# Stick-breaking branch: the fp16 split of a chunk is written over its own U tile, four U tiles and three hlT tiles in place of three and two

## The chip, the cores and the metric

The kernel runs on one core of one Trainium2 chip. The metric is the time of one execution on the device in microseconds, as the median of several runs. Before the change three runs took 2247.16, 2248.38 and 2257.34 us; the median is 2248.38 us.

## The reference, cut to what matters

```python
def reference(x, ...):                                   # x: (1, 2048, 1024) float32
    h = rmsnorm(x, norm_in_g)
    q_sb, k_sb, v_sb, gate_sb, c_q, c_kv, k_rope, gate_mla, gate_logits = split(h @ w_in)
    # first branch: 8 heads of 64, blocks of 128 queries, strictly causal
    z = q k^T * 64 ** -0.5
    w = exp(log_sigmoid(z) + sum of log_sigmoid(-z) over the keys between s and t)
    o_sb = w @ v
    # second branch (MLA): 8 heads, low-rank q and kv, rope, softmax over chunks of 64
    o_mla = softmax(q_full k_full^T * 96 ** -0.5) @ v_mla
    y = g_sb * ((o_sb * silu(gate_sb)) @ w_o_sb) + g_mla * ((o_mla * silu(gate_mla)) @ w_o_mla)
    return rmsnorm(x + y @ w_out, norm_f_g)
```

The first branch's weight of key s for query t is sigmoid(z_ts) times the product of 1 - sigmoid(z_tj) over the keys j between them. The rows of x are handed over in reverse order, so that this product runs forward.

## The kernel before

Every factor of a matmul is kept as two fp16 halves, hi and lo (hi is the value rounded, lo the rest), and a product is three matmuls: hi*hi, hi*lo, lo*hi. The kernel has these stages.

*Norm.* `norm_x` (line 214) loads a block of 128 rows into a U or a B tile, scales it, splits it into hi and lo and has SP transpose it into `hT` (line 223). The split lies in an `hl` tile for even blocks and in an `hlT` tile for odd ones.

*Heads.* 16 heads follow each other, eight of the first branch (`sb_units`, line 344) and eight of the second (`mla_units`, line 527). Beside them `dense_stream` is advanced: units of 24 matmuls (line 166 to 168) that project x onto the next heads' q, k and v, onto the second branch's low-rank factors, and onto the gates. PLAN says how many units go with a head: 17 with each of the first eight heads, then 8, and 4 with the last.

A head of the first branch has 16 units of 128 queries, and a unit one or two chunks of up to 1024 keys, 24 chunks a head. A chunk passes through these steps:

- TensorE writes the scores z (line 332) into one of two PSUM tiles.
- GpSimd sets U[:, 0] to 1 (line 359); ScalarE writes U = sigmoid(-z) (line 360) and B = sigmoid(z) (line 361).
- `stick`: VectorE scans U to running products (line 364; the second chunk of a unit starts from the last column of the first one's U, `unit["prev"]`) and multiplies B by U (line 367).
- `weigh`: ScalarE casts B to hi (line 370) and VectorE subtracts to get lo (line 371), both into an `hl` tile; SP transposes `hl` into an `hlT` tile (line 278).
- `values`: TensorE multiplies the transposed weights by v (lines 287 to 290), and ScalarE copies the sum out after a unit's last chunk.

The second branch has the same last two steps; its chunk is scaled (line 558), exponentiated (line 568), cast (line 571) and subtracted (line 572).

The code is written so that the steps of several chunks overlap: `second` holds back a chunk's `stick` (or `softmax`) until the next chunk's scores are written, and `third` holds back its `values`. `run_third(keep)` in `weigh` leaves `keep` of them, so with 1 the values of chunk j are written down when chunk j + 2 is split, with 2 when j + 3 is. A planner with a model of the engines' times then orders each engine's instructions and gives each new tile the next free buffer of its tag; an instruction that needs a buffer waits for the last user of the one that it gets.

The tiles of 4 KB a partition: three U, three B, two `hl` and two `hlT` in the pool `un`. After the second branch's projections (in head 4) weights' memory comes free and the pool `more` gives three `hl` and three `hlT` on top, and `weigh` keeps 2 instead of 1; `count` deals the requests to the two pools. Before the last head `more` is closed, and its memory goes to the tail's first tiles.

*Tail.* `gated`, `merge` and `finish` weigh both branches by the gates, multiply by the output matrices and norm. The first `gated(0)` is issued inside the last head, after unit EARLY.

Of the kernel before, what the change touches and what calls it, by code (L numbers as in the profile page):

```python
# [9 lines left out]
F32 = mybir.dt.float32  # L10
# [6 lines left out]
P = 128  # L17
# [12 lines left out]
MASK = -3.0e35  # L30
PLAN = [17] * 8 + [8] * 7 + [4]
SCALES = ("g", 4)
EARLY = 6
LEAD = 7
FIRST = 0

# [1 line left out]
def block_kernel(tc, x, norm_in_g, w_in, w_ck, b_gate, q_norm_g, w_q_up, kv_norm_g, w_kv_up,  # L38
# [11 lines left out]
    with ExitStack() as ctx:  # L50
# [121 lines left out]
        with ExitStack() as tctx:  # L172
# [24 lines left out]
            junk = rows.tile([P, WB], mybir.dt.bfloat16, name="junk", bufs=1)  # L197

            def u_tile():
                return un.tile([P, 1032], F32, name="U", tag="U")  # L200

            def b_tile():
                return un.tile([P, 1024], F32, name="B", tag="B")

            def hl_tile(n):
                count[0] += 1
                pool, bufs = (more[0], 3) if more and count[0] % 5 % 2 == 0 else (un, 2)
                return pool.tile([P, 2048], F16, name="hl", tag="hl", bufs=bufs)[:, 0:2 * n]

            def hlT_tile():  # L210
                pool, bufs = (more[0], 3) if more and count[0] % 5 % 2 == 0 else (un, 2)
                return pool.tile([P, 16, 128], F16, name="hlT", tag="hlT", bufs=bufs)

            def norm_x(i):
                xt = (b_tile() if i % 2 else u_tile())[:, 0:1024]
                SP.dma_start(out=xt, in_=x[i * P:(i + 1) * P, :])
                hl = (hlT_tile().rearrange("p a c -> p (a c)") if i % 2 else hl_tile(1024))
                ssq = sm.tile([P, 1], F32, name="ssq", tag="ssq")
                f = sm.tile([P, 1], F32, name="f", tag="f")
                A.activation(out=hl[:, 0:1024], in_=xt, func=AF.Square, accum_out=ssq)  # L220
                inv_rms(ssq, HS ** -2 / D, EPS * HS ** -2, f)
                split(xt, f, hl[:, 0:1024], hl[:, 1024:2048])
                SP.dma_start_transpose(out=hT[i // 8][:, :, i % 8 * P:(i % 8 + 1) * P], in_=hl)
# [43 lines left out]
                while len(second) > keep:  # L267
                    second.popleft()()

            def weigh(unit, vt, blk0, n, first, last, fill, done):  # L270


                run_third(2 if more else 1)
                hl = hl_tile(n)
                fill(hl[:, 0:n], hl[:, n:2 * n])
                nb = n // P
                t = hlT_tile()
                SP.dma_start_transpose(out=t[:, 0:2 * nb, :], in_=hl)

                def values():  # L280
                    if first:
                        unit["av"] = ps_av()
                    av = unit["av"]
                    with tc.issue_after(last_pe[0].ins):
                        for j in range(nb):
                            v = vt[blk0 // 8][:, blk0 % 8 + j, :]
                            T.matmul(out=av[:, 0:64], lhsT=t[:, j, :], rhs=v[:, 0:64],  # L287
                                     start=(first and j == 0), stop=False)
                            T.matmul(out=av[:, 0:64], lhsT=t[:, j, :], rhs=v[:, 64:128], start=False, stop=False)  # L289
                            T.matmul(out=av[:, 0:64], lhsT=t[:, nb + j, :], rhs=v[:, 0:64],  # L290
                                     start=False, stop=(last and j == nb - 1))
                    if last:
                        done(av)

                third.append(values)
# [48 lines left out]
            def sb_units(h, pre):  # L344
                zc, nzc, of = pre[2:5]
                kt, vt = kv_tiles(qk_d[h // 2][:, h % 2], v_d[h // 2][:, h % 2])
                put = o_group(h * 64)
                for i in range(NB):
                    if i % 4 == 0:
                        qt4 = kvp.tile([P, 3, 4, 128], F16, name="qt", tag="qt", bufs=2)  # L350
                        load_q(qk_d[h // 2][:, 2 + h % 2, i:i + 4], qt4[:, 0], qt4[:, 1])
                    unit = {}
                    cks = chunks(i)
                    for ci, (c0, n) in enumerate(cks):
                        z = ps_z()
                        scores(z, kt, [qt4[:, 0, i % 4, :], qt4[:, 1, i % 4, :]], i + c0 // P, n,
                               strict if ci == 0 else None)
                        U, B = u_tile(), b_tile()
                        G.memset(U[:, 0:1], 1.0)
                        A.activation(out=U[:, 1:n + 1], in_=z[:, 0:n], func=AF.Sigmoid, scale=nzc)  # L360
                        A.activation(out=B[:, 0:n], in_=z[:, 0:n], func=AF.Sigmoid, scale=zc)  # L361

                        def stick(U=U, B=B, n=n, ci=ci, c0=c0, i=i, unit=unit, last=(ci == len(cks) - 1)):
                            V.tensor_tensor_scan(out=U[:, 0:n + 1], data0=U[:, 0:n + 1], data1=U[:, 0:n + 1],  # L364
                                                 initial=unit["prev"] if ci else PS, op0=ALU.mult, op1=ALU.bypass)
                            unit["prev"] = U[:, n:n + 1]
                            V.tensor_tensor(out=B[:, 0:n], in0=B[:, 0:n], in1=U[:, 0:n], op=ALU.mult)  # L367

                            def fill(hi, lo):
                                A.copy(out=hi, in_=B[:, 0:n])  # L370
                                V.tensor_tensor(out=lo, in0=B[:, 0:n], in1=hi, op=ALU.subtract)  # L371

                            weigh(unit, vt, i + c0 // P, n, ci == 0, last, fill, lambda av: put(av, of, i))

                        second.append(stick)
                        run_second(1)
                    yield
# [156 lines left out]
            def mla_units(h, pre):  # L534
# [5 lines left out]
                for i in range(NB):  # L540
# [23 lines left out]
                    def softmax(cks=cks, zs=zs, ls=ls, nb=nb, unit=unit, i=i):  # L564
                        f = sm.tile([P, 1], F32, name="fo", tag="fo")
                        for ci, (c0, n) in enumerate(cks):
                            Z = zs[ci]
                            A.activation(out=Z[:, 0:n], in_=Z[:, 0:n], func=AF.Exp, bias=nb, accum_out=ls[:, ci:ci + 1])  # L568

                            def fill(hi, lo, Z=Z, n=n):  # L570
                                A.activation(out=hi, in_=Z[:, 0:n], func=AF.Copy, scale=PS)
                                V.scalar_tensor_tensor(out=lo, in0=Z[:, 0:n], scalar=PS, in1=hi,
                                                       op0=ALU.mult, op1=ALU.subtract)

                            weigh(unit, vt, i + c0 // P, n, ci == 0, ci == len(cks) - 1, fill,
                                  lambda av: put(av, f, i))
                        if len(cks) == 2:
                            V.tensor_tensor(out=ls[:, 0:1], in0=ls[:, 0:1], in1=ls[:, 1:2], op=ALU.add)
                        V.reciprocal(out=f, in_=ls[:, 0:1])
# [319 lines left out]
```

## Time and profile before

| what | us |
|---|---|
| median of three runs | 2248.38 |
| the profiled execution, its time | 2248.75 |
| its span, first to last instruction | 2247.0 |
| TensorE busy with matmuls | 1893.7 |
| VectorE busy | 1560.2 |
| ScalarE busy | 1236.7 |
| GpSimd busy | 300.0 |

All times below are of the profiled execution, in us from its first instruction. PE is TensorE, DVE VectorE, ACT ScalarE, POOL GpSimd, SP the engine that only issues DMAs; `L287` is line 287. "A <- B" in a list of waits says that A was idle and that the end of B released it. Five stretches are named by letters: A is 112 to 512.6 us (heads 0 to 2 of the first branch), B 512.6 to 862.7 (heads 3 and 4, beside the second branch's projections), C 862.7 to 1181 (heads 5 to 7), D 1181 to 1785 (heads 0 to 6 of the second branch), E 1785 to 1904 (its last head). The tail follows.

### The profile page before, as it was taken

Reading aid. Unit: us, or ns where it says so; the run is one execution under the profiler, and the core shown is the slowest. Engines: PE = TensorE matmul, PEld = TensorE weight load, DVE = VectorE, ACT = ScalarE, POOL = GpSimd, SP = SyncE. Lnnn points to the kernel's source line nnn. Section 1 sums busy time; section 2 is a strip of 40 time slices with the busy share of each in tenths; the row PEclk is TensorE's granted clock in tenths of the full one; section 3 lists DMA queues with packets and bytes.
Section 4 is the critical chain, followed back from the end, with each engine's and each line's share of the span. In section 5 each row is a group of like instructions: output and inputs, shape, how many; then the busy total and the mean of one; then the engine's idle time right before and its main releaser. Section 6 shows DMA issues by size and latency. Waiting matters only on the chain.

```text
span 2247.0 us, 41328 instructions
## 1 busy us (share of the span) xinstructions
PE 1893.7 (84%) x15776; PEld 1107.1 (49%) x15776; DVE 1560.2 (69%) x2692; ACT 1236.7 (55%) x2180; POOL 300.0 (13%) x668
## 2 busy tenths in 40 slices
PE   2978888789767888789898987878899986999997
PEld 1545555455434545456555554545556553444443
DVE  3368878778866869888887765656576766666664
ACT  5446656555655658676765665556565655322221
POOL 1211112111101111111111111111111110000000
PEclk9999999999978999999999999988999997999999
DMA  9988898888989979996879999999999989776752
GB/s 247 225 142 166 160 155 157 149 157 170 193 169 165 189 166 190 144 169 140 165 170 174 192 196 188 194 196 197 163 206 184 243 166 228 211 207 186 203 155 73
DMA packets 923431, 401.63 MB, mean 179 GB/s; under 512 B 860000, under 2 KB 880224, under 8 KB 921184
## 3 DMA queue, kind: packets, MB, share of 16 engines
q1 hardware_dynamic: 900640, 339.72, 77.3%
q0 software_dynamic: 20480, 58.74, 11.1%
q8 instruction: 123, 2.02, 0.4%
q10 hardware_dynamic: 2112, 0.52, 0.2%
q14 instruction: 76, 0.62, 0.1%
HBM read 132.52 MB, written 71.84 MB: 91 GB/s over the span
## 4 chain that ended last, share of the span: by engine, by line
DMA 35%; PE 35%; DVE 14%; issue 7%; ACT 7%; SPq 1%; POOL 0%; DVEq 0%; ACTq 0%; POOLq 0%
DMA hlT<-hl 20%; PE z L332 6%; PE mm L166 5%; DVE U L364 5%; PE mm L167 5%; PE mm L168 4%; DMA rt<-r 3%; DMA utb<-hlb 2%; PE yo L166 2%; DMA wf<-in_w_in_dram 2%; PE yo L167 2%; PE yo L168 2%; DVE B L367 2%; PE av L287 2%; DVE hl L371 2%
## 5 line engine op out<-in xcount | busy, mean ns | idle before, releaser
L166 PE MATMUL mm<-w,hT 128*128 128x384 f16 (+1 forms) x1792 | 594.5, 332 | 68.6 <-ACT w L154 36.9
L167 PE MATMUL mm<-w,hT 128*128 128x384 f16 (+1 forms) x1792 | 594.4, 332 | 1.6 <-DVE w L155 1.5
L168 PE MATMUL mm<-w,hT 128*128 128x384 f16 (+1 forms) x1792 | 593.0, 331 | 0.0
L287 PE MATMUL av<-vt,hlT 128*128 128x64 f16 x2176 | 241.7, 198 | 213.9 <-DMA hlT<-hl 208.9
L364 DVE TENSOR_TENSOR_SCAN U<-U 128x1025 f32<-128x1025 f32 (+3 forms) x192 | 323.8, 1687 | 51.8 <-ACT U L360 51.3
L332 PE MATMUL z<-kt,qt 128*128 128x512 f16 (+3 forms) x1280 | 326.3, 361 | 22.9 <-DMA kt<-qkd 7.1
L287 PEld LDWEIGHTS <-hlT 128*128 128x128 f16 x2176 | 202.8, 101 | 268.6 <-DMA hlT<-hl 250.7
L370 ACT CAST hl<-B 128x1024 f16<-128x1024 f32 (+3 forms) x192 | 153.1, 798 | 226.0 <-DVE B L367 144.7
L166 PEld LDWEIGHTS <-hT 128*128 128x128 f16 x1792 | 179.8, 100 | 162.7 <-issue 29.3
L167 PEld LDWEIGHTS <-hT 128*128 128x128 f16 x1792 | 179.6, 100 | 142.6 <-issue 41.1
L290 PE MATMUL av<-vt,hlT 128*128 128x64 f16 x2176 | 241.1, 198 | 0.0
L289 PE MATMUL av<-vt,hlT 128*128 128x64 f16 x2176 | 241.0, 198 | 0.0
L168 PEld LDWEIGHTS <-hT 128*128 128x128 f16 x1792 | 179.5, 100 | 122.1 <-issue 16.0
L371 DVE TENSOR_TENSOR hl<-B,hl 128x1024 f16<-128x1024 f32 (+3 forms) x192 | 174.1, 908 | 83.2 <-ACT hl L370 82.7
L289 PEld LDWEIGHTS <-hlT 128*128 128x128 f16 x2176 | 202.5, 101 | 17.3 <-issue 1.6
L290 PEld LDWEIGHTS <-hlT 128*128 128x128 f16 x2176 | 202.9, 101 | 0.0
L332 PEld LDWEIGHTS <-qt 128*128 128x128 f16 x1600 | 141.1, 101 | 122.3 <-issue 24.0
L367 DVE TENSOR_TENSOR B<-B,U 128x1024 f32<-128x1024 f32 (+3 forms) x192 | 175.1, 912 | 15.7 <-ACT B L361 0.6
L360 ACT ACTIVATE U<-z,nzc 128x1024 f32<-128x1024 f32 (+3 forms) x192 | 166.5, 867 | 33.8 <-PE z L332 32.1
L361 ACT ACTIVATE B<-z,zc 128x1024 f32<-128x1024 f32 (+3 forms) x192 | 166.6, 867 | 0.0
L568 ACT ACTIVATE U<-U,nb 128x1024 f32<-128x1024 f32 (+7 forms) x128 | 98.4, 769 | 108.4 <-DVE nb L562 106.1
L558 DVE TENSOR_SCALAR_CACHE_REDUCE U<-z,mzc 128x1024 f32<-128x1024 f32 (+7 forms) x128 | 104.0, 814 | 60.4 <-PE z L332 59.4
(240 smaller groups left out, 3180.9 us busy)
## 6 DMA issues: line engine op xcount, KB each, us to landing
gd<-go POOLq DMA_DIRECT2D x128, 192.0 KB, 4.8
wf<-in_w_in_dram SPq DMA_DIRECT2D x26, 768.0 KB, 5.6
gt<-gd SPq DMA_DIRECT2D x10, 1024.0 KB, 6.1
qkd<-rt POOLq DMA_DIRECT2D x32, 256.0 KB, 4.2
mqd<-rt SPq DMA_DIRECT2D x32, 256.0 KB, 3.1
qt<-mqd POOLq DMA_DIRECT2D x32, 256.0 KB, 5.4
wf<-in_w_out_dram SPq DMA_DIRECT2D x16, 512.0 KB, 5.8
xt<-in_x_dram SPq DMA_DIRECT2D x16, 512.0 KB, 3.5
```

The lines of the kernel that those rows point to most:

```text
L166: T.matmul(out=ps, lhsT=xh(k), rhs=wh(k), start=(k == 0), stop=False)
L167: T.matmul(out=ps, lhsT=xh(k), rhs=wl(k), start=False, stop=False)
L168: last_pe[0] = T.matmul(out=ps, lhsT=xl(k), rhs=wh(k), start=False, stop=(k == kk - 1))
L287: T.matmul(out=av[:, 0:64], lhsT=t[:, j, :], rhs=v[:, 0:64], start=(first and j == 0), stop=False)
L289: T.matmul(out=av[:, 0:64], lhsT=t[:, j, :], rhs=v[:, 64:128], start=False, stop=False)
L290: T.matmul(out=av[:, 0:64], lhsT=t[:, nb + j, :], rhs=v[:, 0:64], start=False, stop=(last and j == nb - 1))
L332: last_pe[0] = T.matmul(out=z[:, s:s + c], lhsT=st, rhs=half[:, o + s // P:o + (s + c) // P, :].rearrange("p a b -> p (a b)"), start=(a == ...
L360: A.activation(out=U[:, 1:n + 1], in_=z[:, 0:n], func=AF.Sigmoid, scale=nzc)
L361: A.activation(out=B[:, 0:n], in_=z[:, 0:n], func=AF.Sigmoid, scale=zc)
L364: V.tensor_tensor_scan(out=U[:, 0:n + 1], data0=U[:, 0:n + 1], data1=U[:, 0:n + 1], initial=unit["prev"] if ci else PS, op0=ALU.mult, op1= ...
L367: V.tensor_tensor(out=B[:, 0:n], in0=B[:, 0:n], in1=U[:, 0:n], op=ALU.mult)
L371: V.tensor_tensor(out=lo, in0=B[:, 0:n], in1=hi, op=ALU.subtract)
```

## The change

In the first branch a chunk's hi and lo are written over the chunk's own U tile, which has the same size, once the multiply of line 367 has read it. The last column that the next chunk's scan starts from is copied to a small tile first (`pv`). The pool `un` then has four U, three B and three `hlT` tiles and no `hl`. The second branch takes its `hl` tiles from `more` alone (three), and in the last head, where `more` is closed, from the U tiles. `hlT` tiles come from both pools in turn, six in all while `more` is open. `run_third` keeps 2 everywhere. The norm's split lies in `hlT` tiles. EARLY is 7 instead of 6.

```diff
-EARLY = 6
+EARLY = 7
...
             def u_tile():
-                return un.tile([P, 1032], F32, name="U", tag="U")
+                return un.tile([P, 1028], F32, name="U", tag="U", bufs=4)
...
             def hl_tile(n):
+
+                if more:
+                    return more[0].tile([P, 2048], F16, name="hl", tag="hl", bufs=3)[:, 0:2 * n]
+                return u_tile().bitcast(F16)[:, 0:2 * n]
+
+            def hlT_tile():
                 count[0] += 1
-                pool, bufs = (more[0], 3) if more and count[0] % 5 % 2 == 0 else (un, 2)
-                return pool.tile([P, 2048], F16, name="hl", tag="hl", bufs=bufs)[:, 0:2 * n]
-
-            def hlT_tile():
-                pool, bufs = (more[0], 3) if more and count[0] % 5 % 2 == 0 else (un, 2)
+                pool, bufs = (more[0], 3) if more and count[0] % 2 == 0 else (un, 3)
                 return pool.tile([P, 16, 128], F16, name="hlT", tag="hlT", bufs=bufs)
...
-                hl = (hlT_tile().rearrange("p a c -> p (a c)") if i % 2 else hl_tile(1024))
+                hl = hlT_tile().rearrange("p a c -> p (a c)")
...
-            def weigh(unit, vt, blk0, n, first, last, fill, done):
-
-
-                run_third(2 if more else 1)
-                hl = hl_tile(n)
+            def weigh(unit, hl, vt, blk0, n, first, last, fill, done):
+
+
+                run_third(2)
+                if hl is None:
+                    hl = hl_tile(n)
                 fill(hl[:, 0:n], hl[:, n:2 * n])
...
-                            unit["prev"] = U[:, n:n + 1]
+                            if not last:
+                                unit["prev"] = sm.tile([P, 1], F32, name="pv", tag="pv", bufs=3)
+                                V.tensor_copy(out=unit["prev"], in_=U[:, n:n + 1])
                             V.tensor_tensor(out=B[:, 0:n], in0=B[:, 0:n], in1=U[:, 0:n], op=ALU.mult)
...
-                            weigh(unit, vt, i + c0 // P, n, ci == 0, last, fill, lambda av: put(av, of, i))
+                            weigh(unit, U.bitcast(F16)[:, 0:2 * n], vt, i + c0 // P, n, ci == 0, last, fill,
+                                  lambda av: put(av, of, i))
...
-                            weigh(unit, vt, i + c0 // P, n, ci == 0, ci == len(cks) - 1, fill,
+                            weigh(unit, None, vt, i + c0 // P, n, ci == 0, ci == len(cks) - 1, fill,
                                   lambda av: put(av, f, i))
```

## Rows read from the trace of the kernel before

**Rows 1.** Stretches A, C, D, E: length, busy us (count) by engine, PEclk, DMA share, GB/s
```profile
112.00:512.60 400.60, 333.25 (x2881) 202.61 (x2880) 296.67 (x368) 235.36 (x406) 72.19 (x172) 0.93 0.86 156
...
862.70:1181.00 318.30, 282.81 (x2666) 176.63 (x2663) 270.58 (x296) 221.53 (x365) 53.88 (x154) 0.96 0.85 160
1181.00:1785.00 604.00, 516.85 (x5342) 323.49 (x5339) 393.95 (x923) 353.96 (x708) 91.25 (x155) 0.94 1.05 192
1785.00:1904.00 119.00, 93.67 (x829) 54.89 (x828) 76.97 (x154) 67.16 (x107) 9.08 (x16) 0.86 0.89 202
```

**Rows 2.** TensorE's waits, stretches A to E in order: total us, times, longest
```profile
PE av L287 <- DMA hlT<-hl: 51.8, 30, 7.2
...
PE av L287 <- DMA hlT<-hl: 16.1, 5, 7.9
...
PE av L287 <- DMA hlT<-hl: 31.1, 17, 6.4
...
PE av L287 <- DMA hlT<-hl: 85.3, 41, 11.4
...
PE av L287 <- DMA hlT<-hl: 24.7, 11, 5.3
```

**Rows 3.** ScalarE's waits for a split's tile, stretches A, D, E in order
```profile
ACT hl L370 <- DMA hlT<-hl: 69.2, 26, 7.2
...
ACT hl L571 <- DMA hlT<-hl: 18.1, 8, 8.7
...
ACT hl L571 <- DMA hlT<-hl: 25.6, 13, 4.2
```

**Rows 4.** One chunk's steps: ns min/median/max, first and last start us, forms
```profile
L360 ACT ACTIVATE U<-z,nzc x192: 351/992/1199, 117.5 to 1181.0; 128x1024 f32<-128x1024 f32 x80, 128x896 f32<-128x896 f32 x16, 128x768 f32<-128x768 f32 x16, 128x640 f32<-128x640 f32 x16
L364 DVE TENSOR_TENSOR_SCAN U<-U x192: 415/1890/2372, 118.7 to 1181.6; 128x1025 f32<-128x1025 f32 x80, 128x897 f32<-128x897 f32 x16, 128x769 f32<-128x769 f32 x16, 128x641 f32<-128x641 f32 x16
...
L361 ACT ACTIVATE B<-z,zc x192: 354/992/1195, 118.6 to 1181.3; 128x1024 f32<-128x1024 f32 x80, 128x896 f32<-128x896 f32 x16, 128x768 f32<-128x768 f32 x16, 128x640 f32<-128x640 f32 x16
L367 DVE TENSOR_TENSOR B<-B,U x192: 280/1022/1227, 121.1 to 1182.2; 128x1024 f32<-128x1024 f32 x80, 128x896 f32<-128x896 f32 x16, 128x768 f32<-128x768 f32 x16, 128x640 f32<-128x640 f32 x16
L370 ACT CAST hl<-B x192: 284/930/1117, 122.3 to 1182.5; 128x1024 f16<-128x1024 f32 x80, 128x896 f16<-128x896 f32 x16, 128x768 f16<-128x768 f32 x16, 128x640 f16<-128x640 f32 x16
```

**Rows 5.** Line 278's transpositions, stretches C, D, E in order
```profile
DMA to landing us min/median/max: 2.3/5.0/12.8
...
DMA to landing us min/median/max: 2.8/5.4/16.0
...
DMA to landing us min/median/max: 2.3/4.5/8.6
```

**Rows 6.** GpSimd's waits in stretch C: total us, times, longest
```profile
POOL U L359 <- DVE U L364: 99.8, 24, 10.5
```

**Rows 7.** Groups of VectorE, 1181 to 1904: busy, mean ns, idle before
```profile
L579 DVE RECIPROCAL fo<-ls 128x1 f32<-128x1 f32 x128 | 20.3, 160 | 11.4 <-ACT U L568 8.6 <-ACT ot L305 1.3
```

**Rows 8.** The second branch's casts, from U tiles: stretch D, then stretch E
```profile
L571 ACT ACTIVATE hl<-U x112: 293/674/1047, 1189.8 to 1775.6; 128x1024 f16<-128x1024 f32 x14, 128x896 f16<-128x896 f32 x14, 128x768 f16<-128x768 f32 x14, 128x640 f16<-128x640 f32 x14
...
L571 ACT ACTIVATE hl<-U x16: 294/674/1042, 1785.0 to 1889.8; 128x1024 f16<-128x1024 f32 x2, 128x896 f16<-128x896 f32 x2, 128x768 f16<-128x768 f32 x2, 128x640 f16<-128x640 f32 x2
```

**Rows 9.** TensorE's waits in the norm stage, 0 to 112
```profile
PE mm L166 <- DMA hT<-hl: 0.9, 2, 0.7
```

**Rows 10.** The first merge's matmuls, ns and first and last start
```profile
L166 PE MATMUL mm<-WHL,uta x16: 379/379/634, 1857.2 to 1876.1; 128*128 128x512 f16 x16
```

**Rows 11.** Timeline in D: start, us, instruction, [idle before <-releaser]; ScalarE, then TensorE
```profile
1441.45 0.94 ACT L571 ACTIVATE hl<-U 128x896 f16<-128x896 f32 x1
1442.29 1.05 ACT L571 ACTIVATE hl<-B 128x1024 f16<-128x1024 f32 x1
...
1450.89 0.20 PE L287 MATMUL av<-vt,hlT 128*128 128x64 f16 x1 [2.55 <-DMA hlT<-hl]
...
1457.80 0.20 PE L287 MATMUL av<-vt,hlT 128*128 128x64 f16 x1 [1.23 <-DMA hlT<-hl]
```

## The prediction

> **What bounds the kernel now.** I read the stretch table first: four stretches A to E lie between the input norm and the tail (B, the projections of the second branch, is left out of the table and read in the waits). In it the reader is to see that TensorE is the busiest engine in every stretch and that its idle time is the thing to be won: A has 400.60 - 333.25 = 67 us idle (16.8%), C 35.5 us (11.2%), D 87 us (14.4%), E 25 us (21%); VectorE is at 74%, 85%, 65% and 65% [rows 1]. Then TensorE's waits: nearly all of that idle time ends with the landing of a transposition hlT<-hl, just ahead of the value matmuls of line 287: 51.8 us in A, 16.1 in B, 31.1 in C, 85.3 in D, 24.7 in E [rows 2]. Then ScalarE's waits, to see whether it is a buffer or a latency: where there are two hl tiles (A and E) the cast of line 370 or 571 waits for the transposition two chunks back, 69.2 us in A and 25.6 us in E; in D, with five tiles, 18.1 us [rows 3]; in C, with five as well, that view lists none. So A and E are short of tiles and short of lag; C and D are short of lag alone.
>
> A and C do the same chunks (72 each) with 17 dense units a head. What sets them apart is the lag (values stay back by two chunks in A, by three in C, since run_third keeps 1 or 2) and the tiles. C is therefore the row of what A can become.
>
> **The change part by part.** I sum against the profiled execution: its span is 2247.0 us and its time 2248.75 us, 0.37 us above the median of the three runs (2248.38), so a difference carries over as it is.
>
> *Stretch A (heads 0 to 2): lag and tiles.* The split moves into the chunk's own U tile, so the cast waits for no transposition; a fourth U tile is waited for instead, a chunk earlier in the list but with twice the distance (four chunks back, not two). With three hlT tiles the values stay back one chunk more. One chunk lasts 400.6 / 72 = 5.6 us [rows 1], and the 30 waits of TensorE average 1.7 us with a longest of 7.2 [rows 2], so almost all of them fit into the added lag. But C has that lag already and still waits 31.1 us [rows 2]. I take C's idle share for A: 333.25 / (1 - 0.112) = 375 us against 400.6, **-25 us**. The ends are 0 and the whole wait, -52. What is late next is VectorE: 296.67 us of work in 375 us is 79%, under C's 85% [rows 1], so it does not stop the gain.
>
> *Stretch B (heads 3 and 4, with the second branch's projections).* Same edit, but only five waits of 16.1 us [rows 2], and the projections' own chains in between. A third to all of it can go: **-6 us** (0 to -16).
>
> *Stretch C: U becomes the ring.* Before, a U tile was free after the multiply; now it is held until its transposition has landed. By the medians the hold is 0.99 + 0.99 (both sigmoids) + 1.89 (scan) + 1.02 (multiply) + 0.93 (cast) + 1.02 (the subtract, of the multiply's shape) [rows 4] + 5.0 to land [rows 5] = 11.8 us, without queues. Four tiles at a pace of 318.3 / 72 = 4.4 us a chunk allow 17.7 us, so queues may add 5.9 us before ScalarE's sigmoid stalls. The memset of line 359 is the instruction that gets the wait; queued behind it on GpSimd are the DMAs of lines 252 and 254 and the gates' gd (line 607), and ScalarE's copy into the next go tile waits for those. GpSimd already waits at that memset, 99.8 us for the scan alone, without anyone late behind it [rows 6]. I take **+3 us** for bursts; the ends are 0 and TensorE's wait in C once more, +31. In A the ring has 4 x 5.6 = 22 us and costs nothing.
>
> *The prev copies.* 64 more VectorE instructions on 128x1 (8 heads, 8 units with two chunks). The nearest row is a 128x1 reciprocal at 160 ns [rows 7]: 64 x 0.16 = 10 us of work, between scan and multiply, of which VectorE's idle 15 to 26% hides most: **+2 us** (0 to +10).
>
> *Stretch D (heads 0 to 6 of the second branch): five hl tiles become three.* Here the change takes away. 168 casts (7 heads of 24 chunks) start from 1189.8 to 1775.6 us, one every 3.51 us [rows 8], so three tiles keep up as long as a tile is held under 10.5 us. E shows a ring that is really bound: two tiles, 24 casts from 1785.0 to 1889.8 [rows 8], one every 4.56 us, so a hold of 9.1 us; it lands in 4.5 us (median) where D lands in 5.4 [rows 5], so D's hold is about 10.0 us. That is 95% of what three tiles carry, and the second branch casts two chunks back to back, so some casts must wait. How much of it reaches TensorE no row shows. The lower end is below zero: the sixth hlT tile may help the transpositions on SP by a few us (-10). The upper end is the slow rival below (+53). ScalarE is at 354 of 604 us [rows 1] and the values run three chunks behind, which hides most of a late cast, so I stay nearer to the lower end: **+14 us**.
>
> Here the Trainium skill speaks against the change: "Perfetto Trace Analysis", section "Optimization Strategy", says that a gap which keeps coming back on the engine that should be full can mean that memory for the next tile is lacking. By that rule the gaps of A and E are cured by tiles, and D gets them by losing two; it names no price, and the trace agrees in that the wait of rows 3 is 0.96 us a chunk with two tiles and 0.11 with five.
>
> *Stretch E (last head).* hl and the first chunk's scores now share four U tiles, where they had 3 + 2, so the ring of two hl tiles becomes two to three, as the scores leave room; three hlT tiles and one chunk more lag as in A. C's idle share would give 93.67 / 0.888 = 105 against 119, -14; one tile less in all can take as much away. I take **-4 us** (-14 to +12).
>
> *Edits at nothing.* In the norm stage the split has three hlT tiles in place of two and two; TensorE waits 0.9 us for those transpositions beside matmuls [rows 9], so nothing, and that 0.9 us once or twice more if the cover goes. EARLY = 7 puts one step (its loads on SP, its products on VectorE, its sigmoid on ScalarE, its transposition) behind one more unit of head 15, some 4.6 us; its first users, the merge's matmuls, run from 1857.2 to 1876.1 [rows 10] while values go on until about 1890 [rows 8], so nothing, and 4.6 us without that cover. The narrower U (1028) changes no instruction.
>
> Sum: -25 - 6 + 3 + 2 + 14 - 4 = -16 us, from 2248.75 to 2232.75, against the median 2248.38 a time of **2232 us**.
>
> **The rivals.**
>
> *The waits go altogether (2196 us).* If a chunk of lag covers each wait of A, the gain is 52 there, 12 in B and 8 in E, with the other terms as they stand (+19): -53. For it: mean wait 1.7 us against 5.6 us of lag. Against it: C has the lag and keeps 31.1 us of waits [rows 2].
>
> *The stream of transpositions sets the pace (2253 us).* Then tiles and lag only move where the wait is seen: A, B and E gain nothing, D loses nothing as its casts queue for the same stream anyway, and the small costs stay (+5). For it: the DMA engines' share is 0.86 in A and 1.05 in D [rows 1]. Against it: C runs at 0.85 and a pace a fifth faster, and a share can exceed 1, so it is no occupancy. The Trainium skill ("Perfetto Trace Analysis", section "Identifying the Most-Contended Engine") says as much: with 16 DMA engines occupancy misleads, and utilization of the memory is to be read. By the rate, 156 GB/s in A against 202 in E [rows 1], the trace agrees that A has room; by the share alone this rival would be the forecast.
>
> *Three hl tiles bind the second branch (2271 us).* This is the case on the other side. It decides at a hold of 10.5 us, above which each us costs 168 / 3 = 56 us. A cast at 1442.29 had its values at 1457.80, a hold of 15.5 us, the one before, at 1441.45, about 9.4 us [rows 11]: mean 12.4. Midway between 10.5 and 12.4, at 11.45, it is +53 in place of +14, and the whole is +23. For it: holds like that one. Against it: five tiles in flight queue behind each other, three will be held for less, as E's 9.1 shows.
>
> *The change doesn't do what it says.* The planner orders the engines by its own times and may put the values as close to the transposition as today; then about 2250.
>
> **How the numbers follow.** Chances: forecast 0.47 (its own range 2218 to 2246), waits gone 0.17, stream 0.20, three tiles 0.13, nothing done 0.03. A measurement of this kernel tells about 0.5%, 11 us, from no change, so faster means under 2237 and slower over 2259.6. Faster: 0.36 of the forecast and 0.17, 0.53. Slower: 0.11 of the tile case and 0.02 of the stream, 0.13. Same: 0.34. The range 2192 to 2268 cuts about half of the first rival's and half of the third's cases, 0.15 in all.
>
> **What would show it.** In A: ScalarE's cast waiting for hlT<-hl gone, TensorE's wait at line 287 down from 51.8 to about 30 and the stretch 25 us shorter. In C: GpSimd's memset waiting for a DMA, the stretch within 5 us of 318. In D: ScalarE's cast waiting well over 18.1 us, the stretch 5 to 25 us longer; if it grows by 50, the third rival holds. If A keeps its length although the cast's wait is gone, the stream or the planner is the answer. I am wrong altogether if the planner's new order moves other work, dense units above all, across the stretches.

## The result and the profile after

The changed kernel takes 2281.53 us (median of 4 runs, 2270.83 to 2286.59) against 2248.27 of the kernel before beside it: ratio 1.0141 [1.01, 1.0182]. It is slower by 1.4%, where 2232 us and a range up to 2268 had been forecast. The profiled run took 2281.66 us, its span is 2279.9.

To compare stretch by stretch, both traces are cut here at the same events rather than at round times: first sigmoid of head 0, of head 3, of head 5, first cast of the second branch, first cast of its last head, last value matmul. First the kernel before (from, to, length; busy us and count of TensorE, its weight loads, VectorE, ScalarE, GpSimd; granted clock, DMA share, GB/s): norm stage, A, B, C, D, E, tail.

```profile
0.00:117.50 117.50, 71.70 (x396) 40.65 (x397) 43.33 (x93) 62.85 (x106) 25.34 (x52) 0.96 1.05 238
117.50:512.50 395.00, 327.65 (x2845) 199.29 (x2843) 295.46 (x366) 233.07 (x403) 68.90 (x168) 0.93 0.85 154
512.50:862.70 350.20, 281.78 (x2257) 169.75 (x2254) 265.21 (x527) 206.31 (x409) 42.78 (x110) 0.92 0.90 177
862.70:1189.70 327.00, 291.40 (x2730) 181.22 (x2728) 276.33 (x310) 226.54 (x375) 56.37 (x158) 0.96 0.86 161
1189.70:1785.00 595.30, 508.26 (x5274) 318.89 (x5275) 388.19 (x908) 348.95 (x699) 88.76 (x150) 0.94 1.05 192
1785.00:1896.60 111.60, 86.27 (x804) 51.93 (x803) 73.51 (x149) 63.97 (x104) 9.08 (x16) 0.87 0.88 195
1896.60:2247.00 350.40, 326.66 (x1488) 145.40 (x1486) 218.21 (x342) 95.02 (x92) 8.78 (x16) 0.98 0.64 178
```

The same seven stretches of the kernel after:

```profile
0.00:113.60 113.60, 60.17 (x318) 33.67 (x319) 41.66 (x90) 61.15 (x104) 22.30 (x49) 0.94 1.03 226
113.60:504.20 390.60, 338.62 (x2911) 206.39 (x2910) 298.22 (x393) 233.12 (x402) 71.23 (x168) 0.93 0.86 159
504.20:861.40 357.20, 288.66 (x2332) 176.09 (x2329) 269.42 (x553) 212.14 (x422) 51.95 (x114) 0.92 0.90 179
861.40:1185.60 324.20, 283.38 (x2654) 176.77 (x2652) 273.50 (x324) 222.25 (x366) 55.88 (x156) 0.96 0.81 158
1185.60:1808.70 623.10, 514.78 (x5237) 320.02 (x5236) 382.58 (x903) 347.12 (x695) 87.10 (x148) 0.92 1.00 180
1808.70:1908.90 100.20, 85.26 (x827) 51.48 (x825) 63.67 (x133) 55.04 (x96) 10.19 (x18) 0.97 0.98 213
1908.90:2279.90 371.00, 330.32 (x1514) 147.40 (x1510) 234.39 (x364) 105.64 (x100) 8.81 (x16) 0.96 0.63 176
```

Length, and length minus TensorE's busy time, give a ledger. Span: norm -3.9, A -4.4, B +7.0, C -2.8, D **+27.8**, E -11.4, tail **+20.6**, in all +32.9. Idle time of TensorE: norm +7.6, A -15.4, B +0.1, C +5.2, D +21.3, E -10.4, tail +16.9, in all +25.3. Up to the end of C the two kernels have issued the same 3685 dense matmuls, and the kernel after is there 4.1 us sooner; everything lost is lost behind it.

Where the waits went (total us, times, longest). Kernel after: A (first five lines), B (three), C (three), D (three), E (two), tail (one).

```profile
POOL U L362 <- DMA hlT<-U: 188.4, 56, 9.8
PE av L290 <- DMA hlT<-U: 30.6, 18, 5.7
ACT U L363 <- DMA hlT<-U: 19.2, 5, 6.6
PE mm L166 <- DVE r L161: 9.0, 4, 4.9
PE z L335 <- ACT B L364: 6.7, 5, 2.6
...
PE z L335 <- DVE rt L424: 20.7, 7, 11.5
PE z L166 <- ACT B L364: 11.8, 4, 7.4
PE av L290 <- DMA hlT<-U: 4.3, 2, 2.3
...
POOL U L362 <- DMA hlT<-U: 185.7, 58, 10.3
PE av L290 <- DMA hlT<-U: 30.4, 15, 7.0
ACT U L363 <- DMA hlT<-U: 25.4, 10, 6.5
...
ACT hl L577 <- DMA hlT<-hl: 147.1, 74, 14.0
PE av L290 <- DMA hlT<-hl: 98.4, 42, 10.9
PE z L335 <- DMA kt<-mkd: 6.7, 1, 6.7
...
ACT U L577 <- DMA hlT<-U: 19.8, 9, 5.1
PE av L290 <- DMA hlT<-U: 13.3, 12, 2.2
...
PE y L166 <- DMA w<-w: 20.7, 1, 20.7
```

In A the line that bound the kernel before is as forecast: values 30.6 us against 51.8 [rows 2], and the cast's wait of 69.2 [rows 3] is gone. In D the cast's wait grew from 18.1 [rows 3] to 147.1. The last line, in the tail, has no counterpart in the kernel before.

What that last line waits for: SyncE's issue of block 1's load w<-od (its tile is the weight tile that the last dense unit used), the last dense unit on VectorE, and the first matmul that needs the result. Kernel before:

```profile
1857.04 0.62 DVE L605 SCALAR_TENSOR_TENSOR go<-mm,gt,bt 128x384 f32<-128x384 f32 x1
...
1861.06 0.57 SPq L739 DMA_DIRECT2D w<-od  x1
...
1896.37 0.61 PE L166 MATMUL y<-WHL,w 128*128 128x512 f16 x1
```

Kernel after:

```profile
1901.43 0.62 DVE L611 SCALAR_TENSOR_TENSOR go<-mm,gt,bt 128x384 f32<-128x384 f32 x1 [0.37 <-PE mm L168]
...
1903.31 0.58 SPq L745 DMA_DIRECT2D w<-od  x1
...
1934.84 0.61 PE L166 MATMUL y<-WHL,w 128*128 128x512 f16 x1 [20.71 <-DMA w<-w]
```

The chain (load, products, sigmoid, split, transposition) takes 31.5 us in the kernel after. Before, it began 35 us ahead of the last values (1896.6): the last head's own work covered it, and its first matmul waits for nothing. After, the chain begins 5.6 us ahead of the last values (1908.9), so most of it lies open.

### The profile page after: what moved, and what is told of

Same layout as the page of the kernel before. It is cut to its first block, busy times and chain, and to the rows that moved or that the text cites. A ratio compares the mean times of both kernels' runs of the same rounds, so it can differ in the third digit from the quotient of the medians.

```text
span 2279.9 us, 41247 instructions
## 1 busy us (share of the span) xinstructions
PE 1901.2 (83%) x15776; PEld 1111.8 (49%) x15776; DVE 1563.4 (69%) x2756; ACT 1236.5 (54%) x2178; POOL 307.5 (13%) x668
## 4 chain that ended last, share of the span: by engine, by line
PE 26%; DMA 24%; DVE 8%; ACT 4%; issue 4%; SPq 1%; ACTq 0%; DVEq 0%; POOLq 0%; POOL 0%
DMA hlT<-hl 11%; DMA hlT<-U 5%; PE z L335 5%; PE mm L166 2%; PE mm L168 2%; PE mm L167 2%; DVE U L367 2%; PE yo L166 2%; PE yo L168 2%; PE yo L167 2%; PE y L166 2%; PE y L167 2%; PE y L168 2%; DMA utb<-hlb 1%; DMA wf<-in_w_in_dram 1%
## 5 line engine op out<-in xcount | busy, mean ns | idle before, releaser
L335 PE MATMUL z<-kt,qt 128*128 128x512 f16 (+3 forms) x1280 | 332.1, 367 | 59.1 <-DVE rt L424 20.7
L290 PEld LDWEIGHTS <-hlT 128*128 128x128 f16 x2176 | 203.8, 101 | 229.9 <-DMA hlT<-hl 111.6
L167 PEld LDWEIGHTS <-hT 128*128 128x128 f16 x1792 | 180.2, 101 | 151.4 <-issue 51.8
L375 ACT CAST U<-B 128x1024 f16<-128x1024 f32 (+3 forms) x192 | 153.1, 799 | 176.8 <-DVE B L372 175.8
L168 PEld LDWEIGHTS <-hT 128*128 128x128 f16 x1792 | 180.0, 100 | 119.4 <-issue 16.1
L376 DVE TENSOR_TENSOR U<-B,U 128x1024 f16<-128x1024 f32 (+3 forms) x192 | 173.9, 908 | 52.1 <-ACT U L375 51.6
L367 DVE TENSOR_TENSOR_SCAN U<-U 128x1025 f32<-128x1025 f32 (+7 forms) x128 | 173.3, 1355 | 23.9 <-ACT U L363 22.7
L367 DVE TENSOR_TENSOR_SCAN U<-U,pv 128x1025 f32<-128x1025 f32 x64 | 150.4, 2350 | 36.3 <-ACT U L363 32.9
L613 POOL DMA_DIRECT2D gd<-go x128 | 71.1, 555 | 591.1 <-DVE go L611 360.8
```

Source lines behind the costliest of these rows:

```text
L167: T.matmul(out=ps, lhsT=xh(k), rhs=wl(k), start=False, stop=False)
L168: last_pe[0] = T.matmul(out=ps, lhsT=xl(k), rhs=wh(k), start=False, stop=(k == kk - 1))
L290: T.matmul(out=av[:, 0:64], lhsT=t[:, j, :], rhs=v[:, 0:64], start=(first and j == 0), stop=False)
L335: last_pe[0] = T.matmul(out=z[:, s:s + c], lhsT=st, rhs=half[:, o + s // P:o + (s + c) // P, :].rearrange("p a b -> p (a b)"), start=(a == ...
```

## The experiments

The experiments ran in three groups, each beside the kernel before on one chip, and the ratios are to that. Its median was 2242.57 us for e1 to e4, 2241.21 for e5 to e8 and 2229.11 for e9 to e11, so times of different groups are compared by ratio. Stretch lengths are from one profiled run each: kernels whose stretch A holds the same counts of matmuls (e8, e10, e11) took 392.5, 381.5 and 385.6 us for it, so the length of A is read to about 10 us, no closer, and smaller differences are argued from waits.

**EARLY alone: e1 and e2.** The one edit that changes the tail's program, taken out of after and put into before.

```
e1, on after:   -EARLY = 7   +EARLY = 6
e2, on before:  -EARLY = 6   +EARLY = 7
```

> The changed kernel with EARLY = 6 again, nothing else. Changed kernel: one wait of 20.7 us of TensorE in the tail (the merge's matmuls of block 1 wait for a transposition w<-w) and a tail 20.5 us longer than before, counted from the last value matmul. Theory tail-by-EARLY: the later step is what made block 1's chain late; with 6 that wait falls under 3 us and the time comes down by 15 to 20 us, to about 2264. Rival, last-head order: the chain is late because the last head's rows and the last dense unit are late under the new tiles and the new lag, whatever EARLY is; then the wait stays above 12 us and the time stays within 6 us of 2281.

> The kernel before with EARLY = 7 alone. Theory tail-by-EARLY: the tail gets 10 to 20 us longer and the time goes to 2258 to 2268, with a wait of over 8 us for a transposition in the tail. Rival, last-head order: no more than 4 us, 2244 to 2252.

Measured: e1 2269.41 us, 1.0122 [1.0065, 1.0178], tail 372.5; e2 2238.04, 0.9974 [0.9944, 1.0004], tail 350.8. In e1 TensorE still waits 21.6 us for w<-w, in the tail. EARLY costs nothing that shows, as forecast, and the tail's 20 us are not from it.

**Three late hl tiles alone: e3.** The kernel before, with the late tiles for the split cut from five to three and the hlT tiles as they were. Heads 5 to 7 of the first branch use these tiles too, but C shows nothing of it (326.6 us, 327.0 before).

```
-  pool, bufs = (more[0], 3) if more and count[0] % 5 % 2 == 0 else (un, 2)
+  pool, bufs = (more[0], 3) if more else (un, 2)
```

> The kernel before with three hl tiles in place of five while the second branch and heads 5 to 7 run (all from the pool that opens late), hlT as it was. Theory tiles: this alone costs stretch D what the change cost it, 20 to 28 us; ScalarE's wait for hl tiles goes from 18 to over 100 us and TensorE's wait at the values from 85 to about 98; the time goes to 2266 to 2276. Rival, the stream of transpositions sets D's pace: the casts wait but D stays within 6 us and the time at 2246 to 2254, and what the change cost D came from the planner's order.

**Five late hl tiles given back: e4.** The kernel after, with the six late tiles dealt as five hl and one hlT.

```
-  return more[0].tile(..., tag="hl", bufs=3)[:, 0:2 * n]
+  return more[0].tile(..., tag="hl", bufs=5)[:, 0:2 * n]
...
-  pool, bufs = (more[0], 3) if more and count[0] % 2 == 0 else (un, 3)
+  pool, bufs = (more[0], 1) if more and count[0] % 4 == 0 else (un, 3)
```

> The changed kernel with the six late tiles dealt as five hl and one hlT, so the second branch has five hl again and four hlT instead of six (first branch: four hlT in heads 5 to 7, too). Theory tiles: D comes back by 20 us or more, ScalarE's wait for hl tiles falls from 147 to under 40 us, time about 2260. Rival, the stream or the planner's order: D moves by less than 8 us and the time stays within 8 us of 2281; should four hlT be too few, the wait moves to the transpositions' issue on SP and D gets longer.

**Four: e9.** The same with four hl and two hlT late tiles.

```
+  ... tag="hl", bufs=4 ...
+  pool, bufs = (more[0], 2) if more and count[0] % 5 % 2 == 1 else (un, 3)
```

> The kernel after, with the six late tiles dealt as four hl and two hlT (three and three in the kernel after, five and one in e4). What is asked: how the length of stretch D (595 us before, 623 after, 586 with five hl) depends on the number of hl tiles. If casts wait for queued transpositions, whose hold has a spread (theory), each tile takes part of the rest: ScalarE's cast wait in D between the 147 of three and the 22 of five tiles, about 55 to 80 us, D at 595 to 605 us, whole time 2245 to 2262 us. If there is a threshold between three and four (a mean hold of 10.5 to 14 us: four tiles carry 4 x 3.51 = 14.0), four are as good as five: cast wait near 25 us, D at 584 to 592, whole time near 2236 us. If it is the number of hlT tiles that matters (rival), D stays over 610.

Measured: e3 2269.64 us, 1.014 [1.0063, 1.0217], as much as the whole change; e9 2249.21, 1.0079 [1.0051, 1.0108]; e4 2234.34, 0.9958 [0.9928, 0.9987], lower than the 2260 expected. The waits in D of e3, e9 and e4, in this order:

```profile
ACT hl L571 <- DMA hlT<-hl: 143.6, 63, 12.4
PE av L287 <- DMA hlT<-hl: 94.8, 40, 11.4
```

```profile
PE av L290 <- DMA hlT<-hl: 81.5, 52, 6.2
ACT hl L577 <- DMA hlT<-hl: 58.5, 34, 8.8
```

```profile
PE av L290 <- DMA hlT<-hl: 72.0, 44, 5.4
ACT hl L577 <- DMA hlT<-hl: 22.1, 16, 3.9
```

D takes 611.2 us in e3 (592.1 in e2, which is the kernel before in D), 623.1 after, 594.1 with four tiles and 585.8 with five. The cast's wait falls step by step, 147 to 58.5 to 22.1, not at a threshold. D's length tells three tiles from five, but not four from five: it is 611 to 623 us in the three profiles with three (e3, e1, after) and 584 to 595 in seven with five (before, e2, e4 to e8; e10 and e11 put more dense work into D). That e9's whole time, 1.0079, lies above e4's says that the fifth tile counts too; e9's profiled run was the fastest of its four (2238.09 us).

e3 shows that the tiles alone cost D 19.1 us, just under the 20 to 28 expected, with 34 dense matmuls fewer in it than in e2; E does those, and is 10.5 us longer. So e3 loses in D and E what the change loses in D and the tail, and that both come to 1.4% is in part chance. Between e4 and after, where D holds nearly the same dense matmuls (1426 and 1419), the tiles cost it 37 us. e4 shows that all else in the change together, the sixth and fifth hlT tile left out, is worth about 0.4% of gain.

**One chunk of lag less in A: e5.** On e4, to ask what the added lag gives. `more` is empty again in the last head, so E gets the old lag back as well.

```
-  run_third(2)
+  run_third(2 if more else 1)
```

> The version with five hl and four hlT tiles (e4_hl5_hlT4) with the old lag until the second branch's projections are done: run_third keeps 1 there, so A has the new tiles without the longer lag. Theory lag: the longer lag is what took TensorE's wait at A's values from 52 to 29 us, so it comes back to 45 or more and A (head 0's first sigmoid to head 3's) gets 10 to 20 us longer. Rival, tiles: the wait was the ring of two hl tiles, so A stays within 5 us and the wait under 36 us; then a shorter lag also frees U and hlT tiles sooner.

Measured 2249.72 us, 1.0037 [1.0004, 1.007]. TensorE's wait for values in A, e5 and then e4:

```profile
PE av L290 <- DMA hlT<-U: 45.5, 25, 8.4
```

```profile
PE av L290 <- DMA hlT<-U: 29.0, 17, 4.2
```

The lag does remove 16.5 us of this wait, but A is 396.1 us against 391.5: about 5 us, less than the 10 to 20 expected and within what one profile can't tell from nothing. The whole time says more: 1.0037 against 0.9958, and against 0.9961 of e8 beside it, some 17 us. Which stretch these lie in, the profiled runs don't show; the ten runs of e5 range from 2233.8 to 2268.02 us.

**The norm stage's tiles: e6.** On e4, the norm's split takes hlT and U tiles in turn, so that it isn't held to the three hlT tiles.

```
-  hl = hlT_tile().rearrange("p a c -> p (a c)")
+  hl = hlT_tile().rearrange("p a c -> p (a c)") if i % 2 else hl_tile(1024)
```

> e4_hl5_hlT4 with the norm's split in an hlT tile and in a U tile in turn, as in the kernel before it was hlT and hl: no longer three hlT tiles alone. Theory norm: the three tiles cost 8 us before head 0 (TensorE idle 54 us there against 46 before; ScalarE waits 15 us for the norm's transpositions); with the turn the idle time returns to 44 to 48 and the time falls by 4 to 8 us. Rival: the idle time comes from the order of the units' splits (TensorE waits for VectorE at line 161, 12.5 us) and stays above 51 us.

Measured 2245.7 us, 1.0023 [0.9989, 1.0056]; the norm stage's idle time stays at 54.4 us (119.0 - 64.56), where after has 53.4 and before 45.8. The expected gain didn't come, so nothing supports that the tile count of the norm's split costs these 8 us. It isn't ruled out either: in e6 TensorE waits 8.3 us for a transposition out of a U tile, a wait that the kernel after doesn't have there.

**Fewer dense units in the last head: e7.** On e4.

```
-PLAN = [17] * 8 + [8] * 7 + [4]
+PLAN = [17] * 8 + [8] * 3 + [9] * 4 + [0]
```

> e4_hl5_hlT4 with the last head's four dense units spread over the four heads ahead of it (PLAN 17 x8, 8 x3, 9 x4, 0). Theory late weights: in the tail block 1 waits for the last dense unit's weight tile, which in the changed kernel is free only 5 us ahead of the last values and was 39 us ahead in the kernel before; with no dense unit left for the last head the single wait of 15 to 21 us for w<-w goes, and tail and last head together get 10 to 20 us shorter, of which D takes some back; time 2222 to 2232. Rival: the chain waits for the rows of the last head's values, not for the weights; then the wait stays above 10 us and the time does not fall.

Measured 2248.72 us, 1.0036 [1.0007, 1.0066], where 2222 to 2232 was expected; tail 371.9, the wait for w<-w 26.1. It didn't move what it meant to: the last dense unit still came 87.6 us into E. PLAN adds up to 196 units in both lists, and 208 are left after the norm stage, so twelve come after the last head in the program whatever their shares. It says nothing on the tail; e10 and e11 are built on this.

**The split of heads 5 to 7 back in hl tiles: e8.** On e4; these heads, all of C, run with the late tiles at hand.

```
-  weigh(unit, U.bitcast(F16)[:, 0:2 * n], ...
+  weigh(unit, None if more else U.bitcast(F16)[:, 0:2 * n], ...
```

> e4_hl5_hlT4 with the first branch's split in the five hl tiles, not over its own U, as soon as the late pool is open (heads 5 to 7). Theory U ring: ScalarE's sigmoid waits 26 us in C for transpositions out of U; that wait goes to under 5 us, but TensorE loses little by it, so C changes by no more than 6 us. Rival: the U ring costs C its waits at the values too; C gets more than 8 us shorter.

Measured 2229.98 us, 0.9961 [0.9939, 0.9984], the same as e4 by the intervals. C takes 324.5 us (324.0 in e4): ScalarE's sigmoid no longer waits for the U ring, the four U tiles in turn (26.1 us in e4), and TensorE's wait for values is the same, in e4 and then e8,

```profile
PE av L290 <- DMA hlT<-U: 30.2, 13, 6.5
```

```profile
PE av L290 <- DMA hlT<-hl: 32.2, 12, 5.5
```

so the U ring's 26 us on ScalarE cost C nothing that shows.

**All dense units asked for sooner: e10 and e11.** On e8, 208 units planned, eight and two of them in the last head.

```
e10: +PLAN = [17] * 8 + [9] * 6 + [10] + [8]
e11: +PLAN = [17] * 8 + [10] * 7 + [2]
```

> The kernel of e8 (five hl and one hlT late, heads 5 to 7 split into the late tiles), with the dense units of the gates asked for sooner: the plan 17 x 8, 9 x 6, 10, 8 has all 208 units by the end of the last head, where 17 x 8, 8 x 7, 4 left twelve to be placed after it. Theory of the tail: what block 1's chain waits for is the weight tile of the last dense unit, which ended 92.7 us into E after and 72.0 before. With twelve units fewer left over the last one ends at 55 to 75 us, the load w<-od is issued 20 us or more earlier, TensorE's wait for w<-w of 15 to 20 us is under 4, and the tail goes from 370 to 350 to 357 us; E may grow by up to 8 us (less fill), D by the twelve units spread over it less the idle that they fill (0 to +15): whole time 2212 to 2232 us. Rival: the tail's 20 us are from something else (the order of loads on SP in the tail): tail stays 365 to 372.

> As e10, with the plan 17 x 8, 10 x 7, 2: nearly all dense units before the last head. Theory of the tail: the wait for w<-w is gone altogether and the tail is 348 to 355 us, but E has too little dense work to cover its waits for transpositions, so E's idle of TensorE grows from 15 to 25 to 40 us. Whole time 2215 to 2240 us, above e10 by 0 to 12. If the tail's loss did not hang on the last dense unit, the tail stays at 365 to 372 as in e4 to e8.

Measured: e10 2228.5 us, 1.001 [0.9988, 1.0032]; e11 2226.95, 0.9989 [0.9963, 1.0015]. Stretches D, E and tail of e8, e10 and e11:

```profile
1178.60:1762.60 584.00, 501.56 (x5241) 313.45 (x5239) 382.59 (x904) 348.25 (x698) 87.68 (x148) 0.96 1.02 194
1762.60:1858.20 95.60, 80.19 (x790) 49.09 (x788) 56.81 (x127) 51.67 (x94) 10.20 (x18) 0.95 0.94 194
1858.20:2228.70 370.50, 335.33 (x1529) 149.54 (x1526) 237.20 (x368) 105.85 (x101) 8.81 (x16) 0.96 0.63 180
```

```profile
1159.50:1769.60 610.10, 521.87 (x5300) 324.71 (x5298) 391.31 (x907) 350.75 (x698) 88.34 (x152) 0.94 1.03 189
1769.60:1879.70 110.10, 80.46 (x773) 49.00 (x772) 73.50 (x149) 63.94 (x102) 8.00 (x14) 0.88 0.88 187
1879.70:2224.30 344.60, 326.18 (x1489) 145.52 (x1486) 218.76 (x342) 95.03 (x92) 8.78 (x16) 0.99 0.64 181
```

```profile
1168.50:1781.30 612.80, 539.67 (x5463) 336.60 (x5462) 395.20 (x915) 350.21 (x699) 93.12 (x158) 0.95 1.03 193
1781.30:1873.40 92.10, 62.54 (x609) 35.70 (x608) 67.80 (x136) 60.35 (x101) 4.68 (x8) 0.78 0.93 189
1873.40:2220.20 346.80, 325.85 (x1489) 145.85 (x1486) 220.76 (x348) 95.35 (x93) 8.78 (x16) 0.98 0.63 179
```

The theory of the tail holds: with the last dense unit at 76.5 us into E (e10) and 6.9 (e11) the wait for w<-w, 15.2 us in e8, is gone and the tail is 344.6 and 346.8 us. But nothing is won: D, E and tail together take 1050.1, 1064.8 and 1051.7 us. The units that no longer fill E are done in D, which grows by 26 and 29 us, and TensorE is idle for 29.6 us of E in both, 15.4 in e8. For e10 I had expected at most 15 us more in D and 8 in E; they were 26 and 14.5. Its 2228.5 us lie in the range named only because this chip is faster: the kernel before takes 2229.11 on it. e11 was expected no faster than e10; the two are the same by their intervals.

## Why the prediction was wrong

**D, five tiles to three: +14 forecast, +28 measured. This is the step that failed.** Giving the tiles back (e4) takes the whole from 1.0141 to 0.9958 and D from 623.1 to 585.8 us, so by that pair the term is 37. The mechanism was right: casts wait for a tile. What was mis-sized is the price of a ring near its limit, not the hold, the time from a cast's start until its tile is free. I took a hold of 10.0 us against 10.5, the limit of three tiles, and read "95%" as "some casts must wait". Followed over all 168 casts of D in the kernel before (cast start to landing of its transposition), the hold averages 10.7 us over the 124 whose landing is recorded; with the other 44 counted up to their first value matmul, by which they must have landed, it is 11.4 at most, and 90 of the 168 are over 10.5. With three tiles it is 9.7 us by the recorded landings and 10.2 at most (after), 9.4 and 9.9 in e3: about the 10.0 that I had forecast. Two more things follow from the same count:
- The hold does shrink with fewer tiles, as I argued: it is at most 11.9 us on average with five (e4), 11.4 with four (e9), 10.2 and 9.9 with three. But not because transpositions in flight queue less: the recorded ones take 5.5 to 6.0 us from issue to landing in all five profiles. What shrinks is ahead of the issue: from the cast's start to the subtract's end 2.8 us before and 2.3 after, from there to the issue 2.2 and 1.4.
- A mean under the limit doesn't free the ring. At 9.7 to 10.2 us a hold and 3.71 us a cast the three tiles are held 87 to 92% of the time, a quarter of the holds is over 11.3 us by the recorded landings, and 74 of 168 casts wait, 147.1 us in all. That the spread of the holds makes them wait is argued from these figures; no run changed the spread alone. E, from which I took the hold, had said as much: its casts were held 8.4 us on average at most, not the 9.1 that I read from a ring that I took for full, and still 13 of 24 waited [rows 3].

The price could have been read per cast from the rows at hand: 69.2 us over 72 casts in A and 25.6 over 24 in E [rows 3] are 0.96 and 1.07 us each, and D after has 147.1 over 168, 0.88.

My reason for staying near the lower end, that lag hides most of a late cast, held: of the 129 us that the cast waits more, TensorE's values see 13 and its idle time 21. But the 129 us stood nowhere in the sum. The rest of D's growth, 6.5 us, is busy time at a granted clock of 0.92 in place of 0.94. The sixth hlT tile gave nothing that shows: e4 and e8, with four in all, have the shortest D. The rule of the Trainium skill that the prediction set against the change ("Perfetto Trace Analysis", section "Optimization Strategy": gaps that keep coming back can mean that memory for the next tile is lacking) agrees with e3, e9 and e4, and 143.6, 58.5 and 22.1 us of waits are the price that it doesn't name.

**A, -25 forecast.** The wait for values fell to 30.6 us as said, and the cast's wait went. Idle time in A fell by 15.4 us, not 25: the U ring, which I held to cost nothing in A, made the sigmoid wait 19.2 us, and TensorE waits for a split and for the second sigmoid (9.0 and 6.7 us) where before 5.4 went to the split. Then the order of the work moved, which I had named as what would make me wrong: 78 of the 391 dense matmuls of the norm stage now come after the first sigmoid, in A (1366 in place of 1289), so A is busier by 11 us, and the norm stage, which lost them, is only 3.9 us shorter. Norm and A together do the same work and are 8.3 us shorter. What holds the norm stage up is open: e6 speaks against the tiles of its split without ruling them out, and the order itself wasn't tried. What the added lag is worth is open between two readings of e5: about 5 us by A's length, some 17 by the whole time, for 16.5 us of wait.

**B, -6 forecast, +7.0.** The wait for values is down from 16.1 [rows 2] to 4.3 us, but the idle time is the same (+0.1): TensorE now waits 20.7 us for the projections' rotations, where it was 4.7, and 11.8 for a sigmoid, where it was 9.6. The 7 us are work: 25 dense and 48 value matmuls more fall into B, and about as many less into C.

**C, +3 and +2 for the copies.** C is 2.8 us shorter with 8.0 us less work in it, so TensorE's idle time grew by 5.2: about right. The memset waits for a DMA, as said, the stretch is within 3 us, and e8 shows that without the U ring it is no shorter. The 64 copies can't be told from nothing.

**E, -4 forecast, -11.4; the tail, nothing forecast, +20.6.** These belong together: -4 and 0 against +9.2. I took E's gain from lag and tiles, and the lag isn't what brought it. e5 has the old lag in E and is as short there, while e10 has the new lag and takes 110.1 us. The row of e5's E:

```profile
1774.10:1871.70 97.60, 79.52 (x795) 49.58 (x793) 58.54 (x128) 52.03 (x95) 10.18 (x18) 0.97 0.90 190
```

In e10, as in the kernel before, E holds 149 instructions of VectorE, block 1's products among them; after and in e5 it holds 133 and 128, and the tail does the rest. So part of what E gained was only moved; what brought the remainder is open. EARLY itself was right at nothing (e1, e2). What I left out, and so put at nothing without a reason, is the second chain ahead of the merge, block 1's: I checked EARLY's chain against the merge's matmuls [rows 10] but not the one that waits for the last dense unit's weight tile. In the kernel before it had 35 us of cover; a shorter E, with 43 dense matmuls more left over from D, took that cover away. e10 and e11 show the link by breaking it.

**The rivals.** "Three hl tiles bind the second branch" (2271 us) names the right ring and, of all the sums, comes nearest to the time, but that nearness is luck. Its condition, a hold over 10.5 us, wasn't met with three tiles, and its +53 in D is almost twice the 28 measured; the gains that it took over from the forecast, and the tail that it lacked as well, make up the rest. "The waits go altogether" fell, as the 30.6 us in A show. "The stream of transpositions sets the pace" is right for A and B in its outcome, almost no gain, but not in its cause, since D does hang on the tiles while a transposition takes about the same time with three as with five. Up to the end of C its sum, about +5, is 9 us off and mine, -26, is 22 off.

**The size of the error.** 33 us measured (profiled spans) against -16: 49. D gives 14 of them, the tail 21, A with the norm stage 17, B 13, C -8 (with the copies), E -7. The ranges of A, D and E hold what was measured; B's was left by 7 us, C's by 3, and the tail had none. The large errors are all to one side: gains were taken from waits on one line, and costs were taken small.

**A version that beats both.** e4 and e8 keep the split in the U tile and give the second branch five hl tiles: 0.9958 [0.9928, 0.9987] and 0.9961 [0.9939, 0.9984] of the time before, 0.4% faster. With five hl tiles the change is a small gain; three hl tiles were its price.

## What to carry to other kernels

Before taking buffers from a ring, follow every use of it through the trace, and set the spread of the holds, not their mean alone, against tiles times pace: here, at 87 to 92% of the limit, the ring already waited at four of ten uses. Where a ring that is short of tiles stands in the same trace, read its wait per use and multiply. A wait taken off one line of the busiest engine is worth what its next item can start sooner, here some 8 of 21 us by one profile of each kernel, so forecast it by a share and not by the wait. And where a stretch ends in a chain that starts when its last filler work is done, list each such chain with its cover: making the stretch shorter eats the cover first.

## What the runs showed of the hardware

- A transposition from SBUF to SBUF took 5.5 to 6.0 us on average from issue to landing in D, over the 85 to 124 of 168 whose landing each profile records, whether three, four or five split tiles were in use (after and e3, e9, before and e4); the longest recorded took 17.6 us (e3). I had expected it to shorten with fewer in flight.
- The granted clock of E was 0.97 with TensorE busy for 85.26 us of 100.2 (after), 0.87 with 86.27 of 111.6 (before) and 0.78 with 62.54 of 92.1 (e11), so part of the stretch ran at 1.2 GHz in place of 2.4. The busy share alone doesn't give the clock: the norm stage was granted 0.94 with 60.17 us busy of 113.6 (after). In e11's E the matmuls that remain take longer: the 116 of the scores recorded there took 46.8 us in sum, the 110 in e8's E 36.7, 0.40 against 0.33 us each.
